# A two-layer hybrid decoder trunk: feed-forward parts of 6, 6, 6 and 4 tiles, the middle ones' down projection as seven half-width block products

## Chip, core and metric

The kernel runs on one core of a Trainium2 chip. The metric is the device time of one execution in microseconds (us), lower is better. The core has a matrix engine (TensorE, PE in the profile, with its weight loads as PEld), VectorE (DVE), ScalarE (ACT), GpSimd (POOL), the queue engine SyncE (SP), and 16 DMA engines. Matrix results land in eight banks of PSUM, each 512 float32 wide on 128 partitions; everything else lives in SBUF.

## What is computed

The input is one sequence of 512 rows of 1024 features in float32. Each of two layers does this:

```python
x = x + 0.5 * swiglu(rms_norm(x, ffn1_norm[l]), ffn1_w_gate[l], ffn1_w_up[l], ffn1_w_down[l])
h = rms_norm(x, mix_norm[l])
a, g, q, k, v = jnp.split(h @ w_in[l], splits, axis=-1)
conv_out = conv_module(a, g, ...)          # GLU, causal depthwise conv of 31 taps, RMSNorm, swish
diff_out = diff_attention(q, k, v, ...)    # two softmax maps with a bias table, A1 - lam * A2
x = x + jnp.concatenate([conv_out, diff_out], axis=-1) @ w_out[l]
x = x + 0.5 * swiglu(rms_norm(x, ffn2_norm[l]), ffn2_w_gate[l], ffn2_w_up[l], ffn2_w_down[l])

def swiglu(h, w_gate, w_up, w_down):
    return (jax.nn.silu(h @ w_gate) * (h @ w_up)) @ w_down
```

The hidden width of a feed-forward is 2816, that is 22 tiles of 128.

## The kernel before

**Layout.** `x` is kept transposed: 8 tiles (`KT`) of 128 features by 512 positions. Every large product is made in three passes: each factor is split into a high part in float32r and a rest (`parts_of`, lines 95 to 97: ACT makes the high part, DVE or POOL the rest), and `mm3` (157 to 163) adds high x high, high x rest and rest x high into one PSUM bank. Weights come by DMA into a ring of raw tiles (`wraw`, 5), and their parts into rings of 4 (`whi`, `wlo`) with small extra rings of 2 for 512 columns (`RING`, 89).

**A feed-forward** (`ffn`, 392 to 454) goes through `PARTS`, 6, 8 and 8 of the 22 hidden tiles. In each part the gate and up products of all its tiles come first, and then the part's share of the down projection is added to `x`. The first six tiles are computed plainly (`lead_products`, `first_products`, `products`): 48 wide products (512 columns) a tile. For the other 16, `sums` (120) builds sums of weight blocks and `seven` (345) computes a 2 x 2 block product, gate and up by the two halves of the features, with seven block products of 4 x 3 half products (256 columns) instead of eight; `Halves` (304) holds the sums of the normalised input (th, tl). In `seven` the four results a, d (one bank) and c, b (another) are built up in two banks, and intermediate values are copied out by ACT into `keep` (367, 371, 376). The last block, `go(a, "g1u1", "t3")`, is in `rest()` and is issued inside the next tile's `seven` (`before()`, 369), or after the last tile. `gated` (398) splits a hidden tile into hh and hl. The down projection (442 to 454) takes for each of 8 output tiles the part's hidden tiles in turn, three wide products each, in the two banks "mm"; `gather` (105) loads eight 128 x 128 blocks at a time; DVE adds half of the bank to `x` (452). In the last part `after(m)` makes the next norm's input from the finished tile (`Prep.tile`, 249).

**The mixer** (514 to 800): input projections, convolution by taps on DVE (`conv_taps`, 630) with one tile's taps shared by POOL and ACT, attention in 16 steps, output projection. It adds a bias table, `bias`, [128, 4, 512], to the scores (line 691). `make_bias` (459) makes that table once, from a small matrix product, by way of two DRAM tiles: d1 is copied 128 times into d2 (473), and a skewed read of d2 fills `bias` (475), all on POOL's DMA queue. `make_scalars` (480) makes the small constants of both layers, among them lambda, from `lamv` loaded on POOL's queue (483). `aside` (807) calls first `make_bias`, then `make_scalars`, at the fifth tile of the first feed-forward.

**Order.** A scheduler places the instructions of each engine ahead of time: it goes by readiness in its own model of time and, among the ready ones, by the order in the code. `tc.keep_in_program_order(mm)` pins a PE instruction behind the PE instruction written just before it; in `go` (355) the first product of every block is pinned so. The products of the down projection are not pinned. Waits follow from reads and writes; within PSUM they go by bank: as compiled, the first product of b in `seven` waits for ACT's copy of c, which is the other half of the same bank. `pair_banks` (299) hands out the six banks "sc", "po" and "mm" two at a time.

## Time and profile before

| what | value |
|---|---|
| time, median of 3 runs (lowest, highest) | 1823.89 us (1823.62, 1824.05) |
| span of the profiled execution, first to last instruction | 1822.3 us |
| instructions | 27888 |
| moved by DMA | 227.01 MB, mean 125 GB/s |

The profiled execution's time is not listed apart from its span; the span lies 1.6 us below the median of the runs. The page's second part cuts the span into 40 slices of 45.6 us; a digit is the busy share of a slice in tenths, and for PEclk the clock granted to PE:

```profile
PE   8899999999999999999999999999999999999999
PEld 6779999888779889999888998998887888998997
DVE  6757547558876857647567574665688588574662
ACT  5536436445764436436434463554458444363551
POOL 3024024149943023124110241322698420231320
PEclk9999999999999999999999999999999999999999
```

Rows that are shown below have these forms. In a table of instructions: line, engine, operation, out<-in, shape, count | busy us, mean ns of one | idle time before, and what ended it. In a timeline: start, duration, engine, line, and in brackets the idle time before and what ended it. In a table of stretches: from:to, length, busy us (and count) of PE, PEld, DVE, ACT and POOL, then PE's granted clock, the share of the DMA engines, GB/s. A matmul's row lasts longer than its share of the engine, since they are pipelined: spacing is read from starts.

### The profile page before, as it was taken

To read this page: it belongs to the slowest core of one execution; us is meant where nothing else is said; L and a number is where in the kernel's file an instruction comes from. 1 tells how busy PE (TensorE), PEld (TensorE's weight loads), DVE (VectorE), ACT (ScalarE), POOL (GpSimd) and SP (SyncE) were. 2 spreads that over 40 slices of the span, in tenths; PEclk is the share of its full clock that TensorE was granted. 3 is DMA by queue.
4 is the path that set the end of the run, shared out by engine and by line. 5 is a ranking of instruction groups with operands and counts; after the bars stand their busy time and mean duration, and the time that the engine had idled before them with its cause. 6 is when DMAs were issued, how large, how long until landed. Compare 5 with 4: busy or idle time off the path is not lost.

```text
span 1822.3 us, 27888 instructions
## 1 busy us (share of the span) xinstructions
PE 1794.2 (98%) x10692; PEld 1586.2 (87%) x10692; DVE 1201.3 (66%) x1854; ACT 886.2 (49%) x1452; POOL 623.2 (34%) x431
## 2 busy tenths in 40 slices
PE   8899999999999999999999999999999999999999
PEld 6779999888779889999888998998887888998997
DVE  6757547558876857647567574665688588574662
ACT  5536436445764436436434463554458444363551
POOL 3024024149943023124110241322698420231320
PEclk9999999999999999999999999999999999999999
DMA  6346546422213347546423564563231123564561
GB/s 225 128 99 191 150 129 178 134 92 83 81 35 94 98 105 191 149 126 184 132 90 108 133 175 132 151 185 99 77 99 64 47 94 113 134 175 133 151 173 48
DMA packets 105238, 227.01 MB, mean 125 GB/s; under 512 B 11559, under 2 KB 29238, under 8 KB 105104
## 3 DMA queue, kind: packets, MB, share of 16 engines
q1 hardware_dynamic: 85824, 188.78, 31.9%
q0 software_dynamic: 18992, 36.28, 11.6%
q8 instruction: 84, 1.38, 0.3%
q14 instruction: 50, 0.41, 0.1%
q10 hardware_dynamic: 288, 0.16, 0.0%
HBM read 223.07 MB, written 3.42 MB: 124 GB/s over the span
## 4 chain that ended last, share of the span: by engine, by line
PE 92%; DVE 4%; DMA 1%; issue 1%; ACT 1%; DVEq 0%; ACTq 0%
PE ps_pair L362 35%; PE ps_d L159 9%; PE ps_d L162 9%; PE ps_d L163 9%; PE ps_pair L163 5%; PE ps_pair L162 5%; PE ps_pair L159 5%; PE ps_pair L570 2%; PE ps_pair L569 2%; PE ps_pair L571 2%; PE ps_out L159 1%; PE ps_out L162 1%; PE ps_sc L687 1%; PE ps_out L163 1%; DMA lamv<-in_lamv 1%
## 5 line engine op out<-in xcount | busy, mean ns | idle before, releaser
L96 ACT ACTIVATE whi<-wraw 128x512 fp32r<-128x512 f32 (+1 forms) x580 | 458.8, 815 | 670.5 <-PE ps_d L162 231.4
L97 DVE TENSOR_TENSOR wlo<-wraw,whi 128x512 fp32r<-128x512 f32 (+1 forms) x536 | 509.0, 972 | 208.5 <-ACT whi L96 204.0
L362 PE MATMUL ps_pair<-acth,wlo 128*128 128x256 f32 x1024 | 289.8, 283 | 0.0
L362 PE MATMUL ps_pair<-actl,whi 128*128 128x256 f32 x1024 | 289.8, 283 | 0.0
L362 PE MATMUL ps_pair<-acth,whi 128*128 128x256 f32 x1024 | 289.7, 283 | 0.0
L159 PE MATMUL ps_d<-hh,whi 128*128 128x512 f32 x704 | 274.5, 394 | 8.9 <-DVE x L452 3.6
L162 PE MATMUL ps_d<-hl,whi 128*128 128x512 f32 x704 | 275.7, 392 | 1.5 <-DVE hl L402 1.5
L163 PE MATMUL ps_d<-hh,wlo 128*128 128x512 f32 x704 | 274.6, 391 | 0.0
L137 POOL DMA_DIRECT2D wraw<-in_gu x64 | 77.0, 1203 | 491.1 <-DMA wraw<-in_gu 197.6
L362 PE MATMUL ps_pair<-th,wlo 128*128 128x256 f32 x768 | 217.3, 283 | 0.0
L362 PE MATMUL ps_pair<-tl,whi 128*128 128x256 f32 x768 | 217.2, 283 | 0.0
L362 PE MATMUL ps_pair<-th,whi 128*128 128x256 f32 x768 | 217.2, 283 | 0.0
L159 PE MATMUL ps_pair<-acth,whi 128*128 128x512 f32 x512 | 200.6, 395 | 5.8 <-ACT whi L96 5.8
L162 PE MATMUL ps_pair<-actl,whi 128*128 128x512 f32 x512 | 201.1, 393 | 0.3
L163 PE MATMUL ps_pair<-acth,wlo 128*128 128x512 f32 x512 | 200.3, 392 | 0.7 <-DVE wlo L97 0.7
L362 PEld LDWEIGHTS ps_pair<-actl,whi 128*128 128x128 f32 x1024 | 196.6, 192 | 0.3
L362 PEld LDWEIGHTS ps_pair<-acth,whi 128*128 128x128 f32 x1024 | 196.6, 192 | 0.3
L362 PEld LDWEIGHTS ps_pair<-acth,wlo 128*128 128x128 f32 x1024 | 196.6, 192 | 0.0
L452 DVE SCALAR_TENSOR_TENSOR x<-ps_d,x 128x512 f32<-128x512 f32 x96 | 65.3, 690 | 196.0 <-PE ps_d L163 195.9
L142 POOL TENSOR_TENSOR wraw<-wraw 128x512 f32<-128x512 f32 x64 | 91.0, 1423 | 294.1 <-DMA wraw<-in_gu 253.2
L159 PEld LDWEIGHTS ps_d<-hh,whi 128*128 128x128 f32 x704 | 132.8, 189 | 42.2 <-DVE x L452 9.0
L162 PEld LDWEIGHTS ps_d<-hl,whi 128*128 128x128 f32 x704 | 132.9, 189 | 28.6 <-DVE hl L402 2.0
(173 smaller groups left out, 3311.5 us busy)
## 6 DMA issues: line engine op xcount, KB each, us to landing
wraw<-in_gu SPq DMA_DIRECT2D x108, 512.0 KB, 3.6
wraw<-in_gu SPq DMA_DIRECT2D x200, 256.0 KB, 3.7
wraw<-in_gu POOLq DMA_DIRECT2D x64, 512.0 KB, 5.5
wraw<-in_wqkv SPq DMA_DIRECT2D x24, 512.0 KB, 3.5
wraw<-in_dn SPq DMA_DIRECT2D x52, 192.0 KB, 2.9
wraw<-in_wag SPq DMA_DIRECT2D x16, 512.0 KB, 3.6
wraw<-in_wout SPq DMA_DIRECT2D x16, 512.0 KB, 3.4
wraw<-in_dn SPq DMA_DIRECT2D x24, 320.0 KB, 3.5
```

Source lines behind the costliest of these rows:

```text
L96: S.activation(hi, raw, AF.Copy)
L97: (eng or V).tensor_tensor(out=lo, in0=raw, in1=f32(hi), op=ALU.subtract)
L137: nc.gpsimd.dma_start(two.rearrange("p (b c) -> p b c", b=2), u[:, h[0]].unsqueeze(1).broadcast_to([P, 2, 512]), accum_op=ALU.add)
L142: G.tensor_tensor(more[:, h[0]], two[:, h[1]], whole[:, h[0]], op=ALU.add)
L159: first = T.matmul(ps, wh, xh, start=start, stop=False)
L162: T.matmul(ps, wh, xl, start=False, stop=False)
L163: T.matmul(ps, wl, xh, start=False, stop=stop)
L362: mm = T.matmul(ps, l, r, start=first and i == j == 0, stop=False, skip_group_check=True)
L452: V.scalar_tensor_tensor(x[:, m, :], ps, 0.5, x[:, m, :], op0=ALU.mult, op1=ALU.add)
L569: T.matmul(ps[n], xh[:, t], wh, start=k == 0, stop=False)
L570: T.matmul(ps[n], xh[:, t], wl, start=False, stop=False)
L571: T.matmul(ps[n], xl[:, t], wh, start=False, stop=k == KT - 1)
```

## The change

The 22 tiles are dealt into four parts of 6, 6, 6 and 4. The first is plain as before. The two in the middle are "seven": gate and up as before, but their hidden values go to a new class `Hidden`, which splits each tile and, for each pair of tiles, also makes three half-width sums (th, tl); then for each pair of output tiles m and m + 4, `down_sums` loads the weight blocks and builds their sums on POOL, and `seven_down` computes the 2 x 2 block product by seven products of 3 x 3 half products each. The last part has gate and up by `seven` and a plain down projection. All down projections take their banks in turn from `pair_banks`. `Halves` keeps its eight temporary tiles in the space that `Hidden` uses later. The bias table's last read moves into each mixer, into the mixer's own memory; `make_scalars` comes before `make_bias`. In the convolution the last tap of a tile that DVE does alone writes straight to SBUF, without ACT's copy. `ones` and `ones_r` become one tile.

```diff
-PARTS = ((0, 6), (6, 8), (14, 8))
-PLAIN = PARTS[0][1]
-
-SPACE = 392
+PARTS = (
+    ((0, 1, 2, 3, 4, 5), "first"),
+    ((6, 11, 7, 12, 8, 13), "seven"),
+    ((14, 17, 15, 18, 16, 19), "seven"),
+    ((9, 10, 20, 21), "plain"),
+)
...
-        def rest():
+        def rest(out=None):
             go(a, "g1u1", "t3")
             V.tensor_tensor(d, a, keep[:, 3], op=ALU.add)
             V.tensor_tensor(a, a, keep[:, 1], op=ALU.add)
             us = banks[0].rearrange("p (n c) -> p n c", n=2)
-            V.scalar_tensor_tensor(us, us, -1.0, g, op0=ALU.mult, op1=ALU.mult)
-            return banks[0]
+            to = us if out is None else out.rearrange("p (n c) -> p n c", n=2)
+            V.scalar_tensor_tensor(to, us, -1.0, g, op0=ALU.mult, op1=ALU.mult)
+            return banks[0] if out is None else out
...
+    class Hidden:
...
+        def add(self, mm, rest):
+            j, second = divmod(mm, 2)
+            a, b = slice(0, HS), slice(HS, SEQ)
+            h = tmp.tile([P, SEQ], F32, tag="sq", name="hid")
+            rest(h)
+            if not second:
+                V.tensor_tensor(h[:, b], h[:, a], h[:, b], op=ALU.subtract)
+                self.held = h
+            k = second * self.n + j
+            hi = self.fp.tile([P, SEQ], F32R, tag=f"hh{mm}", name="hh")
+            lo = self.fp.tile([P, SEQ], F32R, tag=f"hl{mm}", name="hl")
+            S.activation(hi, h, AF.Copy)
+            V.tensor_tensor(lo, h, f32(hi), op=ALU.subtract)
+            self.parts[k] = hi, lo
+            if second:
+                ha, hb = self.held, h
+                t = self.fp.tile([P, 3, HS], F32, tag="ht", name="ht", bufs=2)
+                V.scalar_tensor_tensor(t[:, 0], ha[:, b], -1.0, hb[:, b], op0=ALU.mult, op1=ALU.subtract)
+                V.scalar_tensor_tensor(t[:, 1], t[:, 0], -1.0, ha[:, a], op0=ALU.mult, op1=ALU.subtract)
+                V.scalar_tensor_tensor(t[:, 2], t[:, 0], -1.0, hb[:, a], op0=ALU.mult, op1=ALU.subtract)
+                S.activation(self.th[:, :, j, :], t, AF.Copy)
+                V.tensor_tensor(self.tl[:, :, j, :], t, f32(self.th[:, :, j, :]), op=ALU.subtract)
...
+    def down_sums(dn, m, m2, f1, f2):
+
+        c = len(f1) * P
+        h = slice(0, c), slice(c, 2 * c)
+        whole, two, u1, more = ring("wraw"), ring("wraw"), ring("wraw2", 512), ring("wraw")
+        load_blocks(two[:, h[0]], dn, m2, f2)
+        load_blocks(u1[:, h[0]], dn, m2, f1)
+        load_blocks(whole[:, h[0]], dn, m, f1)
+        load_blocks(whole[:, h[1]], dn, m, f2)
+        G.tensor_tensor(two[:, h[1]], two[:, h[0]], u1[:, h[0]], op=ALU.add)
+        G.tensor_tensor(more[:, h[0]], two[:, h[1]], whole[:, h[0]], op=ALU.add)
+        G.tensor_tensor(more[:, h[1]], more[:, h[0]], whole[:, h[1]], op=ALU.add)
+        G.tensor_tensor(u1[:, h[0]], u1[:, h[0]], whole[:, h[0]], op=ALU.add)
...
+    def seven_down(hid, w, banks, fp, m, m2, first):
+
+        a, d = banks[0][:, :HS], banks[0][:, HS:]
+        b, c = banks[1][:, :HS], banks[1][:, HS:]
...
+        def go(ps, wt, xt, js=range(n)):
+            at = hid.get(xt)
+            bank_of = 0 if ps is a or ps is d else 1
+            for i, j in enumerate(js):
+                (wh, wl), (xh, xl) = wpart(w[wt], j), at(j)
+                for l, (s, r) in enumerate(((wh, xh), (wh, xl), (wl, xh))):
+                    mm = T.matmul(ps, s, r, start=bank_of not in begun, stop=False, skip_group_check=True)
+                    begun.add(bank_of)
+                    if i == l == 0:
+                        tc.keep_in_program_order(mm)
+
+        def save(i, ps):
+            S.activation(keep[:, i], ps, AF.Copy, scale=0.5)
+
+        most, rest = (range(n - 1), range(n - 1, n)) if first else (range(n), ())
+        go(c, "u2u1", "t1")
+        save(3, c)
+        go(a, "g1", "b11")
+        save(0, a)
+        go(b, "g2", "b21", most)
+        go(d, "u2", "t4", most)
+        go(c, "all", "b22", most)
+        go(a, "g1u2u1", "t2", most)
+        if rest:
+            go(b, "g2", "b21", rest)
+            go(c, "all", "b22", rest)
+            go(d, "u2", "t4", rest)
+            go(a, "g1u2u1", "t2", rest)
+        save(1, d)
+        save(2, a)
+        halves_of = lambda t: t.rearrange("p (n c) -> p n c", n=2)
+        xm, xn = x[:, m, :], x[:, m2, :]
+        V.scalar_tensor_tensor(xm, banks[1], 0.5, xm, op0=ALU.mult, op1=ALU.add)
+        V.tensor_tensor(halves_of(xm), halves_of(xm), keep[:, 0::2], op=ALU.add)
+        V.tensor_tensor(halves_of(xn), halves_of(xn), keep[:, 1::2], op=ALU.subtract)
+        go(a, "g1u1", "t3")
+        V.scalar_tensor_tensor(halves_of(xn), a.unsqueeze(1).broadcast_to([P, 2, HS]), -0.5, halves_of(xn),
+                               op0=ALU.mult, op1=ALU.add)
...
+                if hid:
+                    f1, f2 = sorted(fs[0::2]), sorted(fs[1::2])
+                    for m in range(KT // 2):
+                        w = down_sums(dn, m, m + KT // 2, f1, f2)
+                        seven_down(hid, w, pair_banks(next(turn)), fp, m, m + KT // 2, m == 0)
+                    continue
...
                 for m in range(KT):
-                    ps = bank("mm", "ps_d")
+                    if m % 2 == 0:
+                        banks = pair_banks(next(turn))
+                    ps = banks[m % 2]
...
-                    if m0 + many == FT:
+                    if kind == "plain":
                         after(m)
...
-        nc.gpsimd.dma_start(bias, skew)
+        table.append(skew)
...
+            bias = mp.tile([P, HEADS, SEQ], F32, tag="bias", name="bias")
+            nc.gpsimd.dma_start(bias, table[0])
...
-                else:
-                    S.activation(ys[c], y, AF.Copy)
...
     def aside():
+        make_scalars()
         make_bias()
-        make_scalars()
```

More of the change, by code (lines that the diff above doesn't have):

```diff
@@ L188, in trunk @@
     make_identity(nc, ident)
-    ones = const.tile([P, P], F32, tag="ones", name="ones")
-    G.memset(ones, 1.0)
-    ones_r = const.tile([P, P + SPACE], F32R, tag="ones_r", name="ones_r")[:, :P]
-    V.tensor_scalar(ones_r, ones, 1.0, None, op0=ALU.mult)
+    ones_r = const.tile([P, P + 8], F32R, tag="ones_r", name="ones_r")[:, :P]
+    V.tensor_scalar(ones_r, ident, 0.0, 1.0, op0=ALU.mult, op1=ALU.add)
+    ones = f32(ones_r)
     mhalf = const.tile([P, 16], F32, tag="mhalf", name="mhalf")
@@ L313, in __init__ @@
             self.whole = []
-            free = [(fp, tag, 1) for tag in ("hh6", "hh7", "hl6", "hl7")]
-            free += [(wp, tag, 2) for tag in ("whi2", "wlo2") for _ in range(2)]
+            four = [fp.tile([P, 4, SEQ], F32, tag=tag, name="hn") for tag in ("yh", "yl")]
+            free = [t[:, n] for t in four for n in range(4)]
             a, b = slice(0, HS), slice(HS, SEQ)
@@ new lines, in load_blocks @@
+    def load_blocks(dst, src, m, fs):
+        n = 0
+        while n < len(fs):
+            half, f = divmod(fs[n], HALF)
+            b, w = m * HALF + f, 1
+            while n + w < len(fs) and fs[n + w] == fs[n] + w and f + w < HALF and (b + w) % 8:
+                w += 1
+            c = b % 8
+            nc.sync.dma_start(dst[:, n * P : (n + w) * P], src[half, b // 8][:, c * P : (c + w) * P])
+            n += w
+    def down_sums(dn, m, m2, f1, f2):
[10 more added lines that the diff above has]
+        G.tensor_tensor(u1[:, h[0]], u1[:, h[0]], whole[:, h[0]], op=ALU.add)
+        w = {}
+        for raw, names in ((two, ("u2", "u2u1")), (whole, ("g1", "g2")), (more, ("g1u2u1", "all")), (u1, ("g1u1",))):
+            two_ = len(names) > 1
+            hi, lo = (ring("whi"), ring("wlo")) if two_ else (ring("whi2", 512), ring("wlo2", 512))
+            e = slice(0, c * len(names))
+            parts_of(raw[:, e], hi[:, e], lo[:, e])
+            for n, name in enumerate(names):
+                w[name] = hi[:, h[n]], lo[:, h[n]]
+        return w
@@ L394, in ffn @@
             r = halves = None
-            for m0, many in PARTS:
+            turn = iter(range(100))
+            for fs, kind in PARTS:
+                many = len(fs)
+                hid = Hidden(fp, many // 2) if kind == "seven" else None
                 hh, held, late = [], [], []
```

49 lines of the change are left out of this document (32 added, 17 removed).

## The prediction

> **What bounds the kernel now.** I read first the page (engines, slices, clock), then the table of who waited for whom on TensorE (PE), then stretches and single instructions around the stages that change. In the waits the columns are total us, times, longest us.
>
> ```profile
> PE 1794.2 (98%) x10692; PEld 1586.2 (87%) x10692; DVE 1201.3 (66%) x1854; ACT 886.2 (49%) x1452; POOL 623.2 (34%) x431
> ...
> PE 92%; DVE 4%; DMA 1%; issue 1%; ACT 1%; DVEq 0%; ACTq 0%
> ```
> ```profile
> PE ps_pair L159 <- ACT whi L96: 5.8, 1, 5.8
> PE ps_d L159 <- DVE x L452: 3.6, 11, 0.3
> PE ps_d L159 <- ACT whi L96: 3.4, 1, 3.4
> PE ps_bias L469 <- DMA oneh<-in_onehot: 2.7, 1, 2.7
> ...
> PE ps_d L162 <- DVE hl L402: 1.5, 1, 1.5
> PE ps_d L159 <- DVE gs L433: 1.2, 1, 1.2
> ...
> PE ps_d L159 <- ACT hh L401: 0.5, 1, 0.5
> ```
>
> The reader is to see that PE never stands still for long: 98% busy, 92% of the chain that ended last, and hardly 28 us of idle time in 1822, half of it at the very start and around the bias table. So two things decide: how many products PE issues at which spacing, and whether the change opens gaps in a stream that has none.
>
> **Term 1, the products.** In two of the four parts of each feed-forward, the down projection of 12 tiles changes from 12 x 8 x 3 = 288 products of 512 columns to 2 parts x 4 pairs x 7 blocks x 3 tiles x 3 = 504 products of 256 columns. Over four feed-forwards: 1152 wide ones go, 2016 half ones come. Gate and up, the six plain tiles and the last four stay as many.
>
> ```profile
> 250.31 76.31 PE ps_pair L362 x636
> ```
> ```profile
> 125.45:201.76 76.31, 76.31 (x637) 76.31 (x637) 54.31 (x79) 45.66 (x81) 27.29 (x18) 1.00 0.64 173
> ...
> 217.33:250.00 32.67, 32.67 (x144) 27.03 (x145) 12.80 (x15) 6.54 (x9) 8.42 (x6) 1.00 0.43 108
> ```
>
> The first row is from the chain in order of time: 636 half products in 76.31 us, 0.120 us each. In the second view (stretch, its us, busy us and count of PE, PEld, DVE, ACT, POOL, clock, DMA) a plain down stage has 144 wide products in 32.67 us, 0.227 each. A half product thus costs 0.529 of a wide one, not 0.5, and one eighth fewer blocks is worth 2016 x 0.120 - 1152 x 0.227 = 241.9 - 261.5 = **-19.6 us**. [...]
>
> **Term 2, a wait inside each pair.** `seven_down` puts seven blocks into two banks: c and b in one, a and d in the other. Its last steps are a += g1u2u1, copy d, copy a, then a += g1u1. Each block's first product is pinned behind the product before it, so the next pair cannot start ahead, and PE stands until ACT has read the bank. In `seven` of before the same copy of a (L376) costs nothing, since the last block is issued inside the next tile. The parts of the wait:
>
> ```profile
> 200.04 0.28 PE L362 MATMUL ps_pair<-acth,wlo 128*128 128x256 f32 x1
> ...
> 200.36 0.60 ACT L371 ACTIVATE keep<-ps_pair 128x512 f32<-128x512 f32 x1 [0.50 <-PE ps_pair L362]
> ```
> ```profile
> 512.01 0.49 ACT L710 ACTIVATE at<-ps_at 128x384 f32<-128x384 f32 x1 [1.62 <-PE ps_at L708]
> ...
> 512.55 0.94 PE L717 MATMUL ps_o<-vv,at 128*128 128x128 f32 x6 [0.20 <-ACT at L710]
> ```
> ```profile
> L96 ACT ACTIVATE whi<-wraw 128x1024 fp32r<-128x1024 f32 x252 | 265.8, 1060 | 431.6 <-PE ps_d L162 196.2 <-PE ps_pair L162 109.4 <-PE ps_pair L362 58.6
> ...
> L376 ACT ACTIVATE keep<-ps_pair 128x256 f32<-128x256 f32 x64 | 23.3, 364 | 0.0
> ```
> ```profile
> 216.36 2.01 ACT L96 ACTIVATE whi<-wraw 128x1024 fp32r<-128x1024 f32 x2 [2.02 <-PE ps_d L162]
> ```
> ```profile
> 217.33 0.50 PE L159 MATMUL ps_d<-hh,whi 128*128 128x512 f32 x1 [0.33 <-DVE x L452]
> 217.67 0.40 PE L162 MATMUL ps_d<-hl,whi 128*128 128x512 f32 x1
> ```
>
> A last product at 200.04 lets an idle ACT start 0.32 us later (0.35 taken, for two copies' semaphores). A copy of 256 columns takes 0.364. Two in a row overlap by 0.11 (two splits of 1.060 in 2.01), so 0.25 + 0.36 = 0.62 for two. From ACT's end (512.50) to PE's start are 0.05. Without a wait PE would have gone on 0.12 after the last product. After a wait the first wide product spaces 0.34 instead of 0.227, 0.11 lost. Together 0.35 + 0.62 + 0.05 - 0.12 + 0.11 = 1.01; with one copy alone 0.25 less, 0.76. Which of them? The copy of d is written after a's block, and d lies in a's bank. In the program before, as compiled, b's first product already waits for the copy of c, the other half of its bank: order is kept by bank, not by half. I therefore take two copies: 32 pairs x 1.01 = **+32.3 us**; ends 0 (first rival) and 32 x 1.85 = 59 (third rival). [...]
>
> The other two copies have cover: c is followed by a's block, a by b's, 9 x 0.120 = 1.08 us each, while the answer takes about 0.32 + 0.385 + 0.05.
>
> Do such gaps slow the clock too?
>
> ```profile
> 84.00:92.00 8.00, 5.86 (x18) 4.41 (x19) 8.00 (x14) 8.00 (x14) 0.92 (x1) 0.79 0.28 100
> ...
> 98.00:125.00 27.00, 27.00 (x111) 21.72 (x112) 11.98 (x14) 5.49 (x7) 6.50 (x5) 0.94 0.37 101
> ```
> ```profile
> 520.00:524.00 4.00, 2.65 (x17) 2.22 (x17) 4.00 (x18) 3.50 (x10) 2.97 (x3) 1.00 0.00 0
> ```
>
> After the waits of 3.4 and 1.5 us in the first feed-forward the granted clock fell: 0.79 over 8 us and 0.94 over 27, 0.21 x 8 + 0.06 x 27 = 3.3 us lost. With 1.35 us idle between 520 and 524 it stayed 1.00. Gaps of 1 us, 7.5 us apart, I cost at nothing more.
>
> **Term 3, the start of each such part.** The last tile's values must pass DVE and ACT before the last third of the first pair.
>
> ```profile
> 210.57 0.28 PE L362 MATMUL ps_pair<-th,wlo 128*128 128x256 f32 x1
> ```
> ```profile
> 210.89 0.43 DVE L384 TENSOR_TENSOR ps_pair<-ps_pair,keep 128x256 f32<-128x256 f32 x1 [4.40 <-PE ps_pair L362]
> ...
> 213.01 0.69 DVE L387 SCALAR_TENSOR_TENSOR ps_pair<-ps_pair,keep 128x512 f32<-128x512 f32 x1
> 214.37 0.69 DVE L402 TENSOR_TENSOR hl<-ps_pair,hh 128x512 fp32r<-128x512 f32 x1 [0.66 <-ACT hh L401]
> ```
> ```profile
> L330 DVE TENSOR_TENSOR tl<-ht,th 128x768 fp32r<-128x768 f32 x16 | 15.0, 954 | 0.0
> ...
> L329 ACT ACTIVATE th<-ht 128x768 fp32r<-128x768 f32 x16 | 12.9, 833 | 1.4 <-DVE ht L328 1.4
> ...
> L328 DVE SCALAR_TENSOR_TENSOR ht<-ht,hn 128x256 f32<-128x256 f32 x16 | 6.4, 425 | 0.0
> ```
>
> Today the value's low part ends at 215.06, 4.49 us after the last product began, one weight split between. New behind it are three sums of 0.425, a split on ACT (0.833) and on DVE (0.954): 2.6 to 3.1 us more, so 6.5 to 7.6. PE has, before it needs them, 42 + 6 products of 0.120, 5.8 us. A stall of 0.7 to 1.8 us; I take 1.0, for some sums run while DVE waits for ACT anyway. 8 parts: **+8 us** (ends 0 and 20).
>
> **Term 4, waits that go.** All down products now rotate over three pairs of banks instead of two banks, so the 11 waits for L452 (3.6 us, and 0.11 restart each) go: **-4.8** (ends 0 and -4.8). What is late next is term 3.
>
> **Term 5, scalars first.**
>
> ```profile
> 57.96 0.58 POOL L483 DMA_DIRECT2D lamv<-in_lamv  x1 [1.59 <-DVE lamp L486]
> ```
> ```profile
> 74.53 0.23 DVE L485 TENSOR_TENSOR lamp<-lamv 128x64 f32<-128x64 f32 x1 [8.84 <-DMA lamv<-in_lamv]
> ```
> ```profile
> d<-d POOLq DMA_DIRECT2D x1, 1280.0 KB, 18.9
> ```
>
> The second small load is issued on POOL's queue behind the 1280 KB copy of the table (18.9 us), lands 16.5 us later, and DVE stands 8.84 us with every split and gate of the first part behind it. PE pays the waits 3.4 + 1.2 + 0.5 + 1.5 = 6.6 us and the 3.3 us of clock above. With the scalars' two loads ahead of the copy DVE's 8.84 us go, more than the 6.6 to be won: **-9.9** (ends -5, if the loads' own landing stays in the way, and -9.9). PE's wait of 2.7 us for the one-hot load stays. The table's read into SBUF (1024 KB) goes to each mixer's start on POOL's queue. It can start when the feed-forward's memory is free, with POOL's root (L203) behind it, which is needed only after five of first_products' steps; the first reader is the attention. Cost nothing.
>
> **Term 6, the last part.** With 4 tiles instead of 8, a model tile's sum takes 12 x 0.227 = 2.72 us of PE, and DVE must, per tile, add it (0.69), make the next norm's low part, and half a split.
>
> ```profile
> L97 DVE TENSOR_TENSOR wlo<-wraw,whi 128x1024 fp32r<-128x1024 f32 x208 | 265.6, 1282 | 46.6 <-ACT whi L96 42.4
> ...
> L252 DVE SCALAR_TENSOR_TENSOR actl<-x,par,acth 128x512 fp32r<-128x512 f32 x48 | 49.9, 1057 | 2.0 <-ACT acth L251 2.0
> ```
>
> 0.69 + 1.06 + 0.64 = 2.4 of 2.72, and the next stage's first splits on top. **+2 us** over three such ends (ends 0 and 8).
>
> **What is hidden.** DVE in the gate stage: 54.31 of 76.31 us is 7.2 of each tile's 10.08; `Hidden` adds half of 0.43 + 3 x 0.425 + 0.954, 1.3: 84%, uncovered only if splits come late. In a pair of 8.6 us DVE has four splits (2688 columns, 3.4 us) and four adds of 0.69, ACT under 5.
>
> ```profile
> L142 POOL TENSOR_TENSOR wraw<-wraw 128x512 f32<-128x512 f32 x64 | 91.0, 1423 | 294.1 <-DMA wraw<-in_gu 253.2 <-DVE ps_pair L379 18.4 <-DVE wlo L97 18.1
> ```
>
> POOL's four sums of 384 columns take 4 x 1.423 x 0.75 = 4.3 us. 768 KB of weights a pair are as many bytes as before, in smaller loads on SP's queue. The four copies that leave the convolution and the shared ones tile lie beside other work. All at nothing; were POOL's sums on the path, a pair would lose less than its own 4.3 us once per part, inside term 3's end.
>
> **Sum.** -19.6 + 32.3 + 8 - 4.8 - 9.9 + 2 = +8.0 us. The profiled span is 1822.3; the median of the runs, 1823.9, lies 1.6 above it, which holds what the span leaves out; I add the sum to both alike: 1830.3 and **1831.9**.
>
> **The rivals.** *The gap is filled* (other side): if other products slip into PE's place at the wait, term 2 is 0, and 1831.9 - 32.3 = 1799.6. For it: the view around 201.6 shows down products among the last tile's blocks, since only a block's first product is pinned. Against: all that follows in this stage hangs on a pinned first product. It decides as soon as the wait per pair falls below (32.3 - 8.0)/32 = 0.76 us. *One copy alone* stands in the way, the copy of d being made while c's block runs: 32 x 0.76 = 24.3, so 1823.9, no change. *A split stands before the copies*:
>
> ```profile
> 203.37 0.28 PE L362 MATMUL ps_pair<-th,wlo 128*128 128x256 f32 x1
> ```
> ```profile
> 203.57 1.06 ACT L96 ACTIVATE whi<-wraw 128x1024 fp32r<-128x1024 f32 x1 [0.34 <-PE ps_pair L362]
> 204.53 0.37 ACT L376 ACTIVATE keep<-ps_pair 128x256 f32<-128x256 f32 x1
> ```
>
> Today the copy starts 1.16 us after the last product instead of 0.32, since ACT had begun a split; if so here, 0.84 x 32 = 27 more: 1859. Against: weights of a pair come free after b's and d's blocks, over 2 us earlier, so those splits should be done. *The part's start is longer*: 2.5 us each (the upper end) and 1.7 of half clock behind it, 8 x 3.2 = 26 more: 1858.
>
> **Chances.** Forecast 0.48 (own range 1824 to 1842), one copy 0.17, split ahead 0.17, long start 0.08, gap filled 0.10. Two runs of this kernel can be told apart from about 0.2%, 3.6 us. Faster: the filled gap, and the lower tails of the forecast and the one copy, 0.18; same 0.20; slower 0.62. The range 1816 to 1860 leaves out the filled gap and the far ends.
>
> **What would show it.** Term 1: some 1900 to 2016 half products under seven_down's line at 0.120. Term 2: a PE wait for ACT's keep, 32 times, about 0.7 to 0.9 us idle. Term 3: PE waits for hidden values 8 times. Term 5: no DVE wait for lamv of 8 us and clock 1.00 from 84 to 125. Wrong would be the forecast if PE's waits for keep are under 0.5 us, or ACT's copies start late.

## The result and the profile after

| kernel | median (lowest to highest) | span of the profiled run | mean granted clock |
|---|---|---|---|
| before | 1823.76 us (1823.47 to 1824.05) | 1822.3 | 0.997 |
| after | 1935.97 us (1931.92 to 1939.97) | 1937.7 | 0.980 |

The changed kernel is slower: ratio 1.0617, 95% interval 1.0597 to 1.0637. The prediction, 1831.9 us, had the sign; its range, 1816 to 1860, doesn't hold the time. 112 us were lost where 8 were forecast.

Line numbers from here on are those of the changed kernel: 479 is the product in `seven_down`, 485 ACT's copy into `keep` there, 98 and 99 the splits of weights, 144 and 145 POOL's weight sums for the gate, 451 to 454 its sums for the down projection, 371 and 376 the gate's copies, 412 and 417 to 421 the low part, the three sums and their split in `Hidden.add`. From the page of the changed kernel come the engines, the shares of the chain that ended last, and the clock by slices:

```profile
PE 1815.1 (94%) x11556; PEld 1642.1 (85%) x11556; DVE 1457.5 (75%) x2150; ACT 987.0 (51%) x1678; POOL 769.4 (40%) x559
...
PEclk9999998999999999999999999999999999999999
...
PE 75%; DVE 11%; issue 4%; ACT 3%; DMA 3%; POOL 2%; SPq 0%; POOLq 0%; DVEq 0%; ACTq 0%
```

TensorE's share of the chain fell from 92% to 75%; DVE, ACT, POOL and DMA, which had about 6% of it together, now have 19%. The table of TensorE's waits (total us, times, longest) says where:

```profile
PE ps_pair L479 <- ACT keep L485: 52.1, 36, 1.8
PE ps_pair L362 <- ACT keep L371: 18.8, 8, 3.5
PE ps_pair L479 <- DVE hl L412: 16.2, 8, 2.3
PE ps_rows L211 <- POOL ssum L261: 7.9, 2, 4.0
PE ps_pair L362 <- ACT keep L376: 6.6, 7, 1.2
...
PE ps_pair L479 <- DVE yl L421: 1.4, 5, 0.3
```

32 of the 36 waits in the first row, 49.7 us of it, stand before the last block of a pair; the other four stand at the start of a part. The timeline shows one of the 32 (start, duration, engine, line; in brackets the idle time before and its releaser):

```profile
790.25 0.28 PE L479 MATMUL ps_pair<-yh,wlo 128*128 128x256 f32 x1
...
790.45 1.06 ACT L98 ACTIVATE whi<-wraw 128x1024 fp32r<-128x1024 f32 x1 [1.25 <-PE ps_pair L479]
...
791.42 0.64 ACT L485 ACTIVATE keep<-ps_pair 128x256 f32<-128x256 f32 x2
...
792.11 0.39 PE L479 MATMUL ps_pair<-yh,whi 128*128 128x256 f32 x1 [1.58 <-ACT keep L485]
...
792.33 0.28 PE L479 MATMUL ps_pair<-yl,whi 128*128 128x256 f32 x1
```

From the last product of the block a += g1u2u1 to the first one of a += g1u1 pass 792.11 - 790.25 = 1.86 us, not 0.12, and the next spaces 0.22, 0.10 more than it should: 1.84 us a pair. Both copies are made together, as forecast; ahead of them stands a weight split.

What moved the span by 1937.7 - 1822.3 = +115.4 us, with 0.10 for the restart after each wait; the clock's loss is an estimate, the span times what the mean clock lacks to 1:

| part | forecast | found | worked out from |
|---|---|---|---|
| products (term 1) | -19.6 | -19.6 | 11556 - 10692 = 864 = 2016 - 1152 products, 0.12 apart |
| wait inside each pair (term 2) | +32.3 | +58.9 | 32 x 1.84 |
| start of each seven part (term 3) | +8 | +21.7 | 16.2 + 1.4 + (52.1 - 49.7), 17 restarts |
| L452 of before (term 4) | -4.8 | -4.8 | no such row |
| scalars first, waits alone (term 5) | -6.6 | -6.6 | those rows are gone; 2.5 for `gs` stands where the one-hot's 2.7 stood |
| next norm's start (term 6) | +2 | +8.1 | 7.9, 2 restarts |
| gate stage's copies L371, L376 | 0 | +26.9 | 18.8 + 6.6, 15 restarts |
| clock | -3.3 | +33.3 | 1937.7 x 0.020 - 1822.3 x 0.003 |
| sum | +8.0 | +117.9 | 115.4 measured |

1.84 is the pair shown; by the mean idle time of the 32 (49.7 / 32 = 1.55) it is 1.81, which takes 1.0 from the sum. The other 1.5 us too many lie within what this count takes too high: the slow clock also where PE stands still, and 0.50 of each stretch at half clock, where the spacing of the half products, 0.213 us between 772 and 776 us and 0.120 at a clock of 1.00, gives 0.44. Not in the count are small waits that changed places in the attention, 4.6 us now and 3.8 before.

The second theme is a chain through POOL. At the end of the gate stage, in one part (timelines of ACT, POOL and PE put in order of time):

```profile
737.25 1.29 POOL L144 TENSOR_TENSOR wraw<-wraw 128x512 f32<-128x512 f32 x1 [5.67 <-DVE ps_pair L384]
...
738.62 2.16 POOL L145 TENSOR_TENSOR wraw<-wraw 128x512 f32<-128x512 f32 x1
...
740.74 0.98 POOL L451 TENSOR_TENSOR wraw<-wraw,wraw 128x384 f32<-128x384 f32 x1
...
741.80 0.99 POOL L454 TENSOR_TENSOR wraw<-wraw,wraw 128x384 f32<-128x384 f32 x1
...
742.83 0.52 ACT L98 ACTIVATE whi<-wraw 128x384 fp32r<-128x384 f32 x1 [5.14 <-POOL wraw L454]
...
743.26 0.58 ACT L371 ACTIVATE keep<-ps_pair 128x512 f32<-128x512 f32 x1
...
743.89 0.39 PE L362 MATMUL ps_pair<-th,whi 128*128 128x256 f32 x1 [2.86 <-ACT keep L371]
```

In ACT's order the split of a down weight's sum (L454's) stands ahead of the gate's copy L371 and waits 5.14 us for POOL, whose first two down sums stand behind the gate's last ones. PE waits 2.86 us for the copy. POOL itself stood idle for 5.67 us before L144: the sums are late because of what they are queued behind, not because POOL is full. The loads that L451 and L454 read landed at 737.9 and 738.1, so by an estimate the two sums, 2 us, could have ended at 740.1 instead of 742.8. That makes 2.7 of the 5.14 us the queue's; most of the rest is the sums' own time.

A part's start shows POOL in another way (DVE's and POOL's timeline):

```profile
762.86 1.02 POOL L454 TENSOR_TENSOR wraw<-wraw,wraw 128x384 f32<-128x384 f32 x1 [3.30 <-DMA wraw<-in_dn]
...
763.27 0.89 DVE L417 SCALAR_TENSOR_TENSOR ht<-hid 128x256 f32<-128x256 f32 x1
...
763.84 1.19 POOL L452 TENSOR_TENSOR wraw<-wraw 128x384 f32<-128x384 f32 x1
...
764.19 1.12 DVE L418 SCALAR_TENSOR_TENSOR ht<-ht,hid 128x256 f32<-128x256 f32 x1
...
765.11 1.05 POOL L453 TENSOR_TENSOR wraw<-wraw 128x384 f32<-128x384 f32 x1
...
765.24 1.21 DVE L419 SCALAR_TENSOR_TENSOR ht<-ht,hid 128x256 f32<-128x256 f32 x1
...
766.37 0.68 DVE L412 TENSOR_TENSOR hl<-hid,hh 128x512 fp32r<-128x512 f32 x1
...
767.10 0.39 PE L479 MATMUL ps_pair<-hl,whi 128*128 128x256 f32 x1 [1.90 <-DVE hl L412]
```

Sums of 256 columns that took 0.425 us in the kernel before (L328) take 0.89 to 1.21. Each ends 0.28 or 0.29 us after a POOL sum ends: 763.88 and 764.16, 765.03 and 765.31, 766.16 and 766.45. Three times in a row DVE's sum lasts until shortly after POOL's is through, and the low part that PE wants (L412) stands behind them. The whole trace has the same: of the 72 sums of L417 to L419, 36 overlap a sum of POOL's, and 35 of these end 0.28 or 0.29 us after one ends; the 36 others take 0.41 to 0.43 us.

The clock, from the table of stretches (PE, PEld, DVE, ACT, POOL, clock, DMA, GB/s):

```profile
766.47:769.88 3.41, 1.84 (x11) 1.43 (x11) 3.10 (x5) 2.72 (x4) 0.00 (x0) 1.00 0.00 0
769.88:773.29 3.41, 2.27 (x10) 2.27 (x11) 2.88 (x4) 1.19 (x4) 0.85 (x1) 0.50 0.45 146
773.29:776.70 3.41, 3.41 (x18) 3.41 (x17) 1.96 (x2) 0.81 (x2) 3.15 (x4) 0.50 0.17 46
...
790.36:793.77 3.41, 1.83 (x16) 1.66 (x15) 2.66 (x3) 2.01 (x4) 2.06 (x1) 1.00 0.97 320
793.77:797.18 3.41, 3.41 (x31) 3.41 (x30) 3.41 (x4) 1.57 (x5) 2.92 (x3) 1.00 0.04 14
```

The steady waits of 1.41 to 1.58 us, 9.4 us apart, cost no clock, as the prediction had it: the one in 790.36:793.77 leaves 1.00 behind it, and none of the 24 in this trace is followed by half clock. But between 765 and 771 the wait of 1.90 for the low part and the first pair's wait of 1.79 for its copies (it ended at 771.02) begin 4 us apart, and the clock is 0.50 for 6.8 us, from 769.88 to 776.70: 18 products in a stretch that is busy throughout (773.29:776.70), where one at 1.00 (793.77:797.18) holds 31.

The stretches are cut where the clock changes. In all 14 traces of this case a spell of half clock inside the span lasts 3.41 us or two or three times that, and all spells of a trace begin on one grid of 3.41 us. Counted by the intervals of that grid, in the 14 traces together: after a full-clock interval in which PE stood still for under 1.25 us the clock stayed at 1.00 (7118 of 7118), after 1.94 us or more it fell to 0.50 (110 of 110), and between these it fell in 50 of 208. After a half-clock interval with over 0.58 us of standstill it stayed at 0.50 (61 of 61), after under 0.25 it rose (151 of 151), and between these it stayed in 6 of 15. In the part shown, the end of the wait for the low part (0.63 us), yl's wait (0.29) and the start of the wait for the copies (0.65) make 1.57 us of standstill in 766.47:769.88 (3.41 - 1.84), and the clock is 0.50 from 769.88 on; the rest of the wait for the copies, 3.41 - 2.27 = 1.14 us, lies in the next interval, and the clock is 0.50 for one more. A standstill of this size did not always go with a fall, as the 50 of 208 say. Ahead of each spell at the eight starts of a seven part, the interval held 1.57 to 2.26 us (in the kernel without the sums, below, the clock fell after the first pair's wait of 1.75 us alone in 5 of the 8 parts). In the changed kernel these eight starts have 54.6 us of half clock, 27 of the 39 us that the clock loses in all (by the same estimate, half of each spell's length).

### The profile page after: what moved, and what is told of

Same layout as the page of the kernel before. It is cut to its first block, busy times and chain, and to the rows that moved or that the text cites. A ratio compares the mean times of both kernels' runs of the same rounds, so it can differ in the third digit from the quotient of the medians.

```text
span 1937.7 us, 30746 instructions
## 1 busy us (share of the span) xinstructions
PE 1815.1 (94%) x11556; PEld 1642.1 (85%) x11556; DVE 1457.5 (75%) x2150; ACT 987.0 (51%) x1678; POOL 769.4 (40%) x559
## 4 chain that ended last, share of the span: by engine, by line
PE 75%; DVE 11%; issue 4%; ACT 3%; DMA 3%; POOL 2%; SPq 0%; POOLq 0%; DVEq 0%; ACTq 0%
PE ps_pair L362 24%; PE ps_pair L479 11%; PE ps_pair L164 9%; PE ps_pair L161 9%; PE ps_pair L165 9%; DVE wlo L99 4%; DMA wraw<-in_gu 2%; DVE actl L253 2%; ACT whi L98 2%; PE ps_pair L706 1%; PE ps_pair L705 1%; PE ps_pair L704 1%; PE ps_out L161 1%; PE ps_out L165 1%; PE ps_out L164 1%
## 5 line engine op out<-in xcount | busy, mean ns | idle before, releaser
L98 ACT ACTIVATE whi<-wraw 128x512 fp32r<-128x512 f32 (+3 forms) x660 | 503.7, 785 | 598.2 <-PE ps_pair L164 181.2
L99 DVE TENSOR_TENSOR wlo<-wraw,whi 128x512 fp32r<-128x512 f32 (+3 forms) x616 | 593.0, 983 | 226.6 <-ACT whi L98 223.6
L362 PE MATMUL ps_pair<-th,whi 128*128 128x256 f32 x768 | 219.8, 286 | 25.4 <-ACT keep L371 18.8
L144 POOL TENSOR_TENSOR wraw<-wraw 128x512 f32<-128x512 f32 x64 | 95.5, 1492 | 306.7 <-DMA wraw<-in_gu 223.3
L362 PEld LDWEIGHTS ps_pair<-th,whi 128*128 128x128 f32 x768 | 147.5, 192 | 29.8 <-ACT keep L371 20.4
L362 PEld LDWEIGHTS ps_pair<-tl,whi 128*128 128x128 f32 x768 | 147.6, 192 | 0.3
L362 PEld LDWEIGHTS ps_pair<-th,wlo 128*128 128x128 f32 x768 | 147.6, 192 | 0.0
L479 PE MATMUL ps_pair<-yh,whi 128*128 128x256 f32 x288 | 89.1, 309 | 49.7 <-ACT keep L485 49.7
L479 PE MATMUL ps_pair<-hl,whi 128*128 128x256 f32 x384 | 114.2, 297 | 16.2 <-DVE hl L412 16.2
L261 POOL TENSOR_TENSOR ssum<-ssum,sq 128x512 f32<-128x512 f32 x42 | 68.1, 1620 | 146.6 <-ACT sq L260 145.2
```

Source lines behind the costliest of these rows:

```text
L98: S.activation(hi, raw, AF.Copy)
L99: (eng or V).tensor_tensor(out=lo, in0=raw, in1=f32(hi), op=ALU.subtract)
L144: G.tensor_tensor(more[:, h[0]], two[:, h[1]], whole[:, h[0]], op=ALU.add)
L261: G.tensor_tensor(self.s, self.s, sq, op=ALU.add)
L362: mm = T.matmul(ps, l, r, start=first and i == j == 0, stop=False, skip_group_check=True)
L479: mm = T.matmul(ps, s, r, start=bank_of not in begun, stop=False, skip_group_check=True)
```

## The experiments

Times are medians; ratios are to the kernel before in runs beside it, with their 95% interval.

**The parts that should win.** The kernel before, with `make_scalars()` called ahead of `make_bias()`:

> The kernel before with one edit, the layer scalars made ahead of the bias table. Theory 1 (DVE's 8.84 us wait for lamv behind the table's copy cost PE its waits and some clock): 10 to 11 us faster than before, 1813 to 1814 us, no DVE wait for lamv over 1 us and PE's clock 1.00 between 84 and 125 us. Rival (the table's chain delays something else by as much): within 2 us of before.

1814.12 us, ratio 0.9947 (0.9932 to 0.9962): 9.7 us, term 5 as sized, and the clock between 84 and 125 us is 1.00. Part of the size is luck: PE's wait of 2.7 us for the one-hot load, which the prediction had stay, went, and a wait of 2.5 us for DVE's `gs` came at the same place.

**The new parts without the seven-block down.**

```diff
-    ((6, 11, 7, 12, 8, 13), "seven"),
-    ((14, 17, 15, 18, 16, 19), "seven"),
+    ((6, 11, 7, 12, 8, 13), "mid"),
+    ((14, 17, 15, 18, 16, 19), "mid"),
```

> The changed kernel with its parts of 6, 6, 6 and 4 tiles, but every down projection plain (the two middle parts keep gate and up by seven blocks; the seven-block down is left out, nothing else). Theory 1 (the whole loss sits in the seven-block down and in what feeds it): scalars and banks win 11 + 4.8 us, four parts cost PE nothing, so about 1808 to 1812 us. Rival (four parts, the shorter last part or the table per mixer cost time by themselves): over 1825 us, with PE waits at the ends of the parts.

1819.77 us, ratio 0.9984 (0.9974 to 0.9993), between the two. So the seven-block down projection itself costs 1935.97 - 1819.77 = 116 us. The 8 to 12 us that theory 1 missed are the row for `ssum` L261, which this kernel has with the same 7.9 us as the changed one: both mixers' first row sums wait 4.0 us for POOL's chain of squares, after a last part of 4 tiles; and the mean clock is 0.995.

**The old parts with the rest of the change** (and with `Halves`' temporary tiles in other places).

```diff
+    (tuple(range(6)), "first"),
+    (tuple(range(6, 14)), "mid"),
+    (tuple(range(14, 22)), "plain"),
...
```

> The changed kernel with the parts of before, 6, 8 and 8 tiles, all down projections plain (scalars first, table per mixer and banks in turn stay). Theory 1 (in the four parts version POOL's norm sums come late at two mixer starts, 4 us each with 1.5 us of clock, because the last part is short): 8 to 11 us under the four parts version, 1808 to 1812 us, no PE wait for ssum. Rival (the table's load in each mixer holds POOL's queue): the waits for ssum stay, 1817 to 1821 us.

**1805.19 us**, ratio 0.9898 (0.9882 to 0.9915): faster than both kernels, and 1% faster than the one before. The `ssum` wait is gone, the clock 1.000. Hence that wait comes with the new parts, and pairs of banks, scalars first and the other small edits together are worth some 19 us, 9.7 of it the scalars.

**The wait inside a pair, from four sides.** First the order of the blocks: c's last block behind the two copies, to cover them.

```diff
-        go(c, "all", "b22", most)
         go(a, "g1u2u1", "t2", most)
...
         save(2, a)
+        go(c, "all", "b22", rest or most)
```

> The changed kernel with one order turned round: in a pair, the block c += all comes after a += g1u2u1 and after the two copies are asked for, so that 9 half products (1.08 us) cover the copies. Theory 1 (PE stands 1.55 us, 32 times, for two copies of ACT behind a split): the wait falls to about 0.5 us, 32 x 1.08 = 35 us less, and some of the 33 us of lost clock comes back: 1885 to 1905 us. Rival (PE waits because ACT or DVE have too much to do in this stage): the wait moves to the next block and the time stays over 1920 us.

1919.17 us in two runs far apart (1908.08 to 1930.26), ratio 1.0526 (1.0455 to 1.0596), between theory 1 and the rival. The trace is of the faster run; why the other took 22 us more is not known (its mean clock, 0.973 against 0.978, is about 10 of them). The waits for the copies fell, though not to nothing:

```profile
PE ps_pair L479 <- ACT keep L485: 18.7, 13, 5.4
```

Second, the last block put into the next pair, as `seven` does it in the gate stage, and only the last pair of a part with c's block at its end:

```diff
+        if before:
+            before()
...
+        def end():
+            go(a, "g1u1", "t3")
...
+        if not last:
+            return end
+        end()
```

> The changed kernel with the last block of each pair (a += g1u1) issued in the next pair, behind its first two blocks (18 half products, 2.16 us), as the gate's blocks do it; the last pair of a part has c last instead. Theory 1: the wait for the copies goes but for one of 0.5 us in each part, 1.84 x 24 + 1.1 x 8 = 53 us less, and most of the lost clock comes back: 1850 to 1880 us; what then remains over before is the gate's last tiles and the hidden values' waits, some 45 us. Rival (load of ACT, DVE or POOL): over 1910 us.

1914.8 us, ratio 1.0504 (1.0483 to 1.0525), the rival's figure.

```profile
PE ps_pair L479 <- ACT keep L485: 37.3, 12, 5.5
```

Eight of the twelve waits, 3.0 to 5.5 us each, stand in the last pair of a part. Here the copies have cover in PE's order and none in ACT's: ACT has the splits of the next part's gate weights in front. Covering the wait moved it there.

Third, the copy of d early, so that one copy is left at the pair's end:

```diff
         go(d, "u2", "t4", most)
-        go(c, "all", "b22", most)
-        go(a, "g1u2u1", "t2", most)
...
         save(1, d)
+        go(c, "all", "b22")
+        go(a, "g1u2u1", "t2")
         save(2, a)
```

> The changed kernel with the copy of d asked for right after d's block, so that c's block covers it and one copy alone stands before the last block of a pair. Theory 1 (PE waits for a split and two copies in turn): each wait is 0.27 us shorter, 32 x 0.27 = 9 us less, 1925 to 1930 us. Rival (the wait is for the split alone, the copies start when it ends whatever they are): no change within 3 us; second rival (the split runs because ACT is idle till then; asked earlier, the copy displaces it): 1.1 us a pair less, 35 us.

1950.42 us (ratio 1.0693), slower still. The steady waits did fall by 0.27, what one copy costs, from 1.41 and 1.58 to 1.14 and 1.30. But the edit also reorders the first pair, whose values come last:

```profile
PE ps_pair L479 <- ACT keep L485: 43.1, 44, 1.3
PE ps_pair L479 <- DVE hl L412: 21.3, 8, 3.2
```

So it confirms the price of a copy; what that alone does to the total it does not show.

Fourth, the copies on DVE (`V.tensor_scalar` in `save`), away from ACT's splits:

> The changed kernel with the four copies of each pair of the seven-block down made by DVE instead of ACT. Theory 1 (before the last block of a pair ACT begins a weight split of 0.85 to 1.06 us, since the tile that it fills comes free with the very product that the copies wait for): DVE has no split at that moment, for its half of the split comes after ACT's; the wait falls from 1.55 us by 0.6 to 0.9 us, 32 x 0.75 = 24 us less, 1905 to 1918 us. Rival (any engine would be late there, because all are full): the wait stays at 1.4 us or more, 1930 us or more.

1961.63 us, ratio 1.0751 (1.0694 to 1.0808). Before the last block the wait is 33.8 us in 32, about 1.06 each: without the split ahead it falls by a third, though not to the 0.7 to 0.9 us that the prediction named. But DVE is late with the other copies, 20 waits before the blocks that follow them, with 31.0 us. What the last block gained, DVE's queue gave back and more: the wait fell as theory 1 said, and the time is the rival's.

**POOL's sums.** The sums left out, and loads of single blocks in the place of three of them, so that the seven blocks no longer add up to the product:

```diff
-        G.tensor_tensor(two[:, h[1]], two[:, h[0]], u1[:, h[0]], op=ALU.add)
-        G.tensor_tensor(more[:, h[0]], two[:, h[1]], whole[:, h[0]], op=ALU.add)
-        G.tensor_tensor(more[:, h[1]], more[:, h[0]], whole[:, h[1]], op=ALU.add)
-        G.tensor_tensor(u1[:, h[0]], u1[:, h[0]], whole[:, h[0]], op=ALU.add)
+        load_blocks(two[:, h[1]], dn, m2, f1)
+        load_blocks(more[:, h[0]], dn, m, f1)
+        load_blocks(more[:, h[1]], dn, m, f2)
```

> The changed kernel without POOL's four sums of down weights in each pair: three more loads put plain blocks in their places (the sums are left out, so the down projection of the two middle parts is not what it should be; products, splits and copies are as many). Theory 1 (POOL's sums come late for ACT's splits, which stand in ACT's queue ahead of the gate's copies, and while they run DVE's work on SBUF is slow): PE's waits for the gate's copies (20.4 + 8.4 us) go, the wait for the last hidden values falls from 2.0 to under 1.2 us a part, half of the lost clock comes back: 1865 to 1885 us. DVE's sums of 256 columns take 0.42 us instead of up to 1.24. Rival (the gate's last tiles and the hidden values wait for ACT's order or for DMA): over 1915 us and the same waits.

1865.41 us, ratio 1.0227 (1.0206 to 1.0247). The waits of this kernel:

```profile
PE ps_pair L478 <- ACT keep L484: 50.1, 32, 1.7
PE ps_rows L211 <- POOL ssum L261: 7.9, 2, 4.0
```

The waits for L371, L376, the low part and yl are gone, all 43.0 us of them, and 2 of those for keep; the 32 waits inside the pairs stay. Of the 70.6 us, these are 45, and their restarts some 3 more; the clock gives 22, for it is 0.991 (1865.9 x 0.009 = 16.8 us lost, 38.8 before). One of DVE's sums, from the groups by form (count | busy us, mean ns | idle before), in the changed kernel and then in this one:

```profile
L418 DVE SCALAR_TENSOR_TENSOR ht<-ht,hid 128x256 f32<-128x256 f32 x24 | 15.6, 650 | 0.3
```
```profile
L418 DVE SCALAR_TENSOR_TENSOR ht<-ht,hid 128x256 f32<-128x256 f32 x24 | 10.0, 418 | 0.3
```

418 ns is near the 425 that such a sum took in the kernel before. So the four sums that the prediction put at nothing cost some 70 us, in ACT's order, in DVE's rate and in the clock; how much of it each of the first two has is not separated, for both go with the sums.

Both edits together, the last block deferred and no sums:

> The same, with the last block of each pair issued in the next pair (the sums are left out here too). If the waits for the copies and POOL's sums are all that the seven-block down costs, the products' 19.6 us show: 1805 to 1835 us, PE's clock above 0.99. Rival (each wait that goes is replaced by another, since the weights of the next part are the real limit): over 1870 us, with PE's waits at the ends of the parts.

1840.96 us, ratio 1.0093 (1.0062 to 1.0124): between theory and rival, and still 0.9% slower than before.

```profile
758.30 0.63 ACT L98 ACTIVATE whi<-wraw 128x512 fp32r<-128x512 f32 x1 [2.29 <-DMA wraw<-in_gu]
759.59 0.63 ACT L98 ACTIVATE whi<-wraw 128x512 fp32r<-128x512 f32 x1 [0.66 <-POOL wraw L144]
761.26 1.15 ACT L98 ACTIVATE whi<-wraw 128x512 fp32r<-128x512 f32 x2 [1.04 <-POOL wraw L145]
762.31 0.64 ACT L484 ACTIVATE keep<-ps_pair 128x256 f32<-128x256 f32 x2
```

This is ACT at a part's end. Its idle times of 2.29, 0.66 and 1.04 us are waits of gate splits for a load and for POOL's gate sums, and the two copies PE wants stand behind them: 26.8 us in 8 waits.

The sums on DVE (`V` for `G`), alone and with the last block deferred:

> The changed kernel with the four sums of down weights of a pair made by DVE instead of POOL, result as it should be. Theory 1 (POOL's sums are the cause: late behind the gate's sums in POOL's queue, and slow for DVE's work on SBUF at the same time): the waits for the gate's copies (L371, 18.8 us) go or halve, DVE's sums of 256 columns take 0.42 us, 1880 to 1910 us, if DVE's 2.1 us more a pair find room in 9.4. Rival (what is late is the loads of the down weights, whoever adds them): DVE stands for the loads and takes splits and gates with it, 1930 us or more.

> Both edits that leave the result whole: the last block of a pair issued in the next one, and DVE's sums in place of POOL's. If each removes its own wait: 1855 to 1885 us (the same with the sums left out ran at 1841). Rival (a pair of 7.6 us has no room for DVE's 8.1 us of splits, adds and sums): PE waits for splits, over 1900 us. Either way it stays behind the version with all down projections plain, 1805 us, by over 50 us.

1929.4 us (ratio 1.0574, 1.0544 to 1.0605) and 1918.6 us (1.0515, 1.0485 to 1.0546): both where their rivals had them, the first 0.6 us short of it. Of DVE's waits in the first:

```profile
DVE wraw L451 <- DMA wraw<-in_dn: 19.9, 12, 3.9
```

The gate's copy L371 is no longer waited for (1.6 us left of 18.8). In its place DVE stands at its first sum for the down weights' load, 19.9 us in 12 waits, and PE waits 10.0 us for the gate weights' low parts and 27.9 for yh, yl and hl. The wait moved with the sums from POOL's queue to DVE's. In the second kernel PE's largest row is not one for splits, as its rival had it, but again the copies in the last pair of a part, 40.5 us in 8 waits.

**Is it the split?** The split at 790.45 started 0.20 us after the last product began; the copies of that bank start 0.31 us after it in the run below, where nothing stands before them. The reason lies in the order of the three products of a tile: its last one reads the weight's low part, so the high part's place came free one product before the bank. One line in `seven_down` changes that order:

```diff
-                for l, (s, r) in enumerate(((wh, xh), (wh, xl), (wl, xh))):
+                for l, (s, r) in enumerate(((wh, xh), (wl, xh), (wh, xl))):
```

> The changed kernel with one line of the seven-block down altered: inside each tile the weight's low part is multiplied second and its high part again last (high x high, low x high, high x low), the same three products. The last product of the block a += g1u2u1 then still reads the weight's high tile, so ACT's next split, which wants that tile's place, no longer comes free one product before ACT's two copies, and the planned order of ACT has the copies first and the split behind them. Theory 1 (the wait inside a pair is 1.86 from last product to next instead of the predicted 1.13 because a split stands before the copies): idle time before the last block falls from 1.41 to 1.58 to 0.85 to 1.0 us, 32 times, so 18 to 22 us less, and 1905 to 1920 us in all, less if the clock's losses shrink too; the gate-stage waits (L371, L376) and those for the hidden values' low part stay. Rival (the split is only moved, and PE waits for its weights at the next block; or the copies are late for another reason): idle time at the last block stays over 1.3 us or comes back as waits for whi or wlo, time over 1930.

1912.21 us, ratio 1.0483 (1.0466 to 1.0501): theory 1, 23.8 us less than the changed kernel. Waits and timeline:

```profile
PE ps_pair L479 <- ACT keep L485: 27.9, 33, 2.0
PE ps_pair L362 <- ACT keep L371: 15.3, 8, 3.2
PE ps_pair L479 <- DVE hl L412: 15.1, 8, 2.1
```
```profile
779.95 0.28 PE L479 MATMUL ps_pair<-yl,whi 128*128 128x256 f32 x1
...
780.26 0.66 ACT L485 ACTIVATE keep<-ps_pair 128x256 f32<-128x256 f32 x2 [1.25 <-PE ps_pair L479]
...
780.81 1.06 ACT L98 ACTIVATE whi<-wraw 128x1024 fp32r<-128x1024 f32 x1
...
780.97 0.39 PE L479 MATMUL ps_pair<-yh,whi 128*128 128x256 f32 x1 [0.75 <-ACT keep L485]
```

The copies start 0.31 us after the last product and the next block 1.02 after it; the prediction's 0.35 + 0.62 + 0.05 was 1.02. The split stands behind them, and PE has no wait for it. Not tried: this order together with the sums elsewhere or the last block deferred.

## Why the prediction was wrong, and where it was right

The steps that failed are three: the rival of the split ahead was turned down (term 2, 26.6 us more), POOL's sums were put at nothing (some 70 us, of which term 3's excess and the gate's copies are parts), and the clock was judged by single gaps (33.3 us lost where 3.3 were to be won).

**Right:** *Term 1* (products, -19.6): the trace has the 864 products more, and those of the new stage start 0.12 apart at a clock of 1.00 where nothing is waited for. *Term 4* (the waits for L452 go): their row is missing. *Term 5* came out at 9.7 of 9.9, with one wait exchanged for another. That the two copies are waited for together, 32 times, is shown by the timelines, and that a copy costs 0.27 by the early copy of d. "Gaps of 1 us, 7.5 us apart, I cost at nothing more" holds for the clock, even for 1.41 to 1.58 us in the steady pairs.

**Term 2, mis-sized: 58.9 instead of 32.3.** The mechanism was right and so was the price without a split (1.02 measured). The step that failed is the rejection of the third rival: "weights of a pair come free after b's and d's blocks, over 2 us earlier, so those splits should be done". It looked at two of the three wide weight tiles. The third, `more` (g1u2u1 and all), is read until that very block, and its place goes to a tile wanted only later; ready 0.12 us sooner than the copies, it was put ahead. The rival's 1.85 a pair was nearly exact (1.84); its chance of 0.17 was too small.

**"All at nothing" for POOL's sums, wrong: some 70 us with its clock.** I counted their 4.3 us against a pair's 8.6 and found room; I costed the busy time and not the order. I missed three things: ACT's queue has a split that wants a sum ahead of a copy that PE wants (L371, 18.8 us); POOL's sums stand behind the gate's own; and 35 of DVE's sums end only just after one of POOL's, up to 1.24 us long instead of 0.42. The sentence "were POOL's sums on the path, a pair would lose less than its own 4.3 us once per part, inside term 3's end" bounded a part's loss at 4.3 us; without the sums PE's waits fell by 45 us in 8 parts, 5.6 each, at two places, the gate's last tiles and the part's start, and the clock's 22 us were not in the bound at all.

**Term 3, mis-sized by the same cause: 21.7 instead of 8.** Without POOL's sums the waits for the hidden values are zero. The working itself was too long: 4.49 + 2.6 is 7.1, not the 6.5 at which its range begins, and in the kernel without the sums the low part of the last tile (L412) ends 4.54 us and the last split (L421) 5.80 us after the last gate product starts, in all 8 parts, just within the 5.8 us of cover. With POOL's sums L412 ends after 7.4 to 8.4 us, behind DVE's sums of up to 1.21 us in the row shown.

**Term 6, mis-sized: 8.1 of waits instead of 2,** with its upper end 8. I counted DVE's 2.4 of 2.72 us for a tile; what was late was POOL's chain of squares for the next norm.

**The clock, wrong: +33.3.** The prediction reasoned on single gaps. In the traces a fall goes with the standstill within one interval of 3.41 us (1.94 us or more: 110 of 110; under 1.25: none of 7118), and over 0.58 us in a half-clock interval goes with another one (61 of 61). The rival of a longer start had 2.5 us of wait and 1.7 of half clock a part, that is one interval. Found were 21.7 / 8 = 2.7 and 27.3 / 8 = 3.4, mostly two intervals. So this rival and the split ahead came true together; each alone would have given 1858 or 1859.

**In sum,** seven blocks save 19.6 / 32 = 0.61 us a pair. With the last block behind the copies that is less than the cheapest wait (0.76 for one copy, by the prediction's rows). Deferring the block takes the wait out of 24 of the 32 pairs, but leaves one of 2.8 us or more at the end of each part. Even with the sums left out as well the kernel stays 17 us above the one before. It does not pay in any form that was run.

## What to carry to other kernels

Work that an engine has time for isn't hidden yet. Look at what stands behind it in that engine's queue, and at what stands behind each instruction that waits for it in another queue: here a split waited 5.14 us for a sum, and behind the split stood a copy that PE wanted. Compare the gain per unit (here 0.61 us a pair) with the least wait that the new structure brings before adding terms. When several instructions become ready at nearly the same time, the order of the last reads (which operand the last product uses) can decide which goes first; here that was one line and 24 us. Add up waits that lie close together before costing the clock: here three waits made 1.57 us of standstill in one interval of 3.41 us, and half clock came after it.

## What the runs showed of the hardware that was not expected

- DVE's sums beside POOL's: in the trace of the changed kernel 36 of the 72 sums of 256 columns (L417 to L419) overlap a sum of POOL's, and 35 of these end 0.28 or 0.29 us after one ends; the longest takes 1.24 us. The other 36 take 0.41 to 0.43 us, and in the run without POOL's sums one of these sums (L418) takes 0.418 us on average.
- The granted clock, counted from its records in the 14 traces of this case: it changed on a grid of 3.41 us inside the span. In the changed kernel none of the 24 steady waits of 1.41 to 1.58 us, 9.4 us apart, is followed by half clock. In the 14 traces an interval with 1.94 us or more of standstill was followed by 0.50 in 110 cases of 110, and a half-clock interval with over 0.58 us of it by another in 61 of 61.
